# Residual gate rows: from VectorE products in the output projection to TensorE chunks in the projection stream

## The chip, the cores and the metric

The kernel runs on one core of a Trainium2 chip. The metric is the time of one execution on the device in microseconds (us); lower is better. The engines are named as in the profile: PE is TensorE (matmuls), DVE is VectorE, ACT is ScalarE, POOL is GpSimd, and SP is SyncE, which here only issues transfers (DMAs). SBUF is the on-chip memory, PSUM the memory that matmuls write, in eight banks.

## The reference

One layer of a hybrid diffusion backbone on 640 tokens (128 context, 512 latent) of 2048 features, all in float32:

```
mod   = silu(c) @ w_mod + b_mod              # 2048 -> 3 x 2048, for c (latent) and c_ctx (context)
shift, scale, gate = split(mod, 3)
h     = rms_norm(x, norm_w) * (1 + scale) + shift
proj  = h @ w_in                             # 640 x 2048 -> 640 x 7216
u_f, z_f, q, k, v, z_d, a, b = split(proj)
y_f   = fourier_mix(u_f) * silu(z_f)         # 4 groups of 128 channels
y_d   = rms_norm(gated_delta(conv(q), conv(k), conv(v), a, b)) * silu(z_d)   # 12 heads of 128, two directions
y     = concat(y_f, y_d) @ w_out             # 640 x 2048 -> 640 x 2048
out   = rms_norm(x + gate * y, final_norm_w)
```

The final states of the scan over the context tokens are an output too. What the change is about is `gate`: two rows of 2048 numbers, one for the latent and one for the context tokens, which are a vector times a third of `w_mod` (2048 x 2048, 16 MB) plus a bias. They are needed only at the very end, where they multiply the output projection.

## The kernel before

Matrices are cut into tiles of 128 partitions. The large products are made in float32r in three passes: each weight tile is split into a rounded part `whi` (ACT, line 135) and a rest `wlo` (POOL, line 136), each activation likewise, and PE computes hi x hi, lo x hi and hi x lo.

The work has four stages. At startup (lines 156 to 440) `x` is transposed and normed, and shift and scale are made by `mod_rows` (line 275): for each of 16 row blocks of `w_mod`, a matmul with 32 columns of weights `cz` (of which two are used, the two conditioning vectors) and 256 columns of `w_mod`, four such side by side in the four column strips of the array by `tile_position=(0, 32 * q)`. A second step adds the four strips.

The projection stream (`stream`, line 976) runs through 50 tiles of 128 columns of `w_in`, 2 x 48 matmuls of 320 tokens each (line 988). Between its chunks the program interleaves, by generators, the steps of the heads: `solve` (line 596) inverts the diagonal 32 x 32 blocks on DVE, with detours through DRAM (`pd`, `NP`, `xd`, `DD`); `delta` (line 701) puts together the whole 128 x 128 inverse and runs the scan with the state `S`; `head_out` multiplies by the gate of the branch; `fourier` does the Fourier groups. The generators are stepped against a clock written out by hand (lines 1284 to 1304): the stream adds 0.82 a step, and a generator yields a latency, after which it is due again, and a busy time. The order so given is a priority: the trace has loads for the next head issued as soon as their buffer is free.

In `delta`, one tile `AL` holds, for both directions and five chunks, the decayed products of keys (index 0, later the inverse) and of keys with queries (index 1). `DD` holds the inverted blocks, spread out over 128 columns with zeros between.

The output projection (`out_stream`, line 1219) has four column groups of 512 columns. Group `n` takes 16 row groups `k` of `w_out` and, for each of five token tiles, three matmuls of 512 columns (line 1252); the fourth group is cut into tokens 0 to 2 and 3 to 4, so that there are five passes, `p` 0 to 4. Pass 0 starts while the last heads finish. Five sums need five of the eight PSUM banks, so passes alternate between `bank` (five) and `mbank` (three). `out_loader` splits weights four row groups ahead; for the first three column groups they come through `raw`, issued by ACT, and for the fourth through `wo`, issued by SP into four buffers of the tag `wg`.

The gates are made here as well. `out_gate` (line 1098) loads, for each column group, four pieces of 1 MB of `w_mod` into the same tag `wg`, multiplies them on DVE by the two vectors, 32 products of 128 x 512 (lines 1108 and 1110), and splits the sums; `finish` adds over the partitions by a matmul with a matrix of ones, which also spreads the result over all partitions. Since the gates come later than the sums of the projection, groups 0 to 2 are copied out of PSUM to `res` by ACT (line 1274), and multiplied, added to `x` and squared later (`out_add`, line 1158), in an order that `out_gates` (line 1181) makes from an estimate of how far DVE has come.

Of the kernel before, what the change touches and what calls it, by code (L numbers as in the profile page):

```python
# [71 lines left out]
def hybrid_step(ctx: ExitStack, tc: tile.TileContext, x_prompt, x_sample, state_ctx, c, c_ctx,  # L72
# [28 lines left out]
    gd = dram.tile([24, NT], F32, name="gd")  # L101
    gb4 = dram.tile([NH, 4, 2, 160], F32, name="gb4")
# [133 lines left out]
        # The scale of the modulation comes first: the gate columns and the keys, values and queries of the first head  # L236
        # are multiplied without the shift, which the tokens share; its product with their columns is added later.
# [204 lines left out]
    # a first result comes back from DRAM, and the product with the shift is added  # L442
# [19 lines left out]
    def gates():  # L462
# [8 lines left out]
        ax, aa, au, lg = [g.tile(W24, F32, tag="ab", name="ab", bufs=4) for _ in range(4)]  # L471
# [48 lines left out]
    YT = g.tile([P, 5, 64], F32, tag="YT", name="YT")  # L520
    TA = g.tile([P, 5, 64], F32, tag="TA", name="TA")
    for x in (YT, TA):
        POOL.memset(x, 0.0)
# [58 lines left out]
    # gates wait in DRAM, in the place of the branch outputs that they will multiply  # L582
# [13 lines left out]
    def solve(h):  # L596
# [67 lines left out]
        YB = g.tile([40, 16, 16], F32, tag="YB", name="YB", bufs=1)  # L664
# [25 lines left out]
        for b in range(4):  # L690
            SP.dma_start(out=DD[32 * b:32 * b + 32, 0:2, :, 32 * b:32 * b + 32].rearrange("p d t c -> p (d t) c"),
                         in_=xd[10 * b:10 * b + 10].rearrange("u r c -> r u c"))
# [6 lines left out]
    LAT = (1, 2, 3, 4)  # L699

    def delta(h):
# [14 lines left out]
        AL = g.tile([P, 2, 5, 2, P], F32, tag="AL", name="AL", bufs=1)  # L716
        for ts in ((0, 1, 2), (3, 4)):
            pk = bank()
            for i, t in enumerate(ts):
                o = toff(t)  # L720
                PE.matmul(pk[:, P * i:P * (i + 1)], lhsT=KT[:, o:o + P], rhs=QT[:, o:o + P], start=True, stop=True)
            for i, t in enumerate(ts):
                E = g.tile([P, 2, P], F32, tag="E", name="E", bufs=2)
                for d in range(2):
                    ACT.activation(E[:, 1 - d], gb[:, d, P * t:P * (t + 1)], AF.Exp, bias=ngg4[:, d, h, t:t + 1])
                DVE.tensor_tensor(AL[:, :, t, 0], s["KK"][:, :, t], E, ALU.mult)
                DVE.tensor_tensor(AL[:, :, t, 1], pk[:, P * i:P * (i + 1)].unsqueeze(1).broadcast_to([P, 2, P]), E,
                                  ALU.mult)
# [5 lines left out]
        def half(x, odd):  # L734
            return x.rearrange("p (m b c) -> p m b c", m=2, b=2)[:, :, odd]

        px = bank()
        for t in range(5):
            for d in range(2):
                for m in range(2):  # L740
                    (o, co), (_, ci) = pairs[2 * m + 1 - d], pairs[2 * m + d]
                    PE.matmul(px[o, 32 * t:32 * t + 32], lhsT=AL[:, 1 - d, t, 0, co], rhs=DI[d][:, t, ci],
                              start=True, stop=True, tile_position=(0, o.start))
        for r, cc in pairs:
            POOL.tensor_copy(AL[r, :, :, 0, cc], DD[r, 1:3, :, cc])
        for b in range(4):
            POOL.tensor_copy(TA[pairs[b][0], :, pairs[b % 2][1]], DD[pairs[b][0], 0 if b < 2 else 3, :, pairs[b][1]])
        pv = px[:, 0:160].rearrange("p (t c) -> p t c", t=5)
        ACT.copy(YT[0:64, :, 0:32], pv[0:64])
        ACT.copy(YT[64:128, :, 32:64], pv[64:128])  # L750
# [6 lines left out]
        pv = px[:, 0:320].rearrange("p (t c) -> p t c", t=5)  # L757
        DVE.transpose(TA[32:64, :, 0:32], pv[0:32, :, 0:32])
        DVE.transpose(TA[64:96, :, 32:64], pv[96:128, :, 32:64])
        for d in range(2):  # L760
            for m in range(2):
                i, o, cc = pairs[2 * d + m][0], pairs[2 * m + d][0], pairs[2 * m + 1 - d][1]
                ACT.copy(AL[o, 1 - d, :, 0, cc], pv[i, :, 32 * m:32 * m + 32])
# [4 lines left out]
        for t in range(5):  # L768
            for d, (ra, rb) in enumerate(((lo, up), (up, lo))):
                PE.matmul(px[rb, 64 * t:64 * t + 64], lhsT=AL[ra, 1 - d, t, 0, rb], rhs=TA[ra, t, :], start=True, stop=True,  # L770
# [4 lines left out]
        for t in range(5):  # L775
            for d, (ra, rb) in enumerate(((lo, up), (up, lo))):
                PE.matmul(px[ra, 64 * t:64 * t + 64], lhsT=ET[rb, t, :], rhs=AL[rb, 1 - d, t, 0, rb], start=True, stop=True,
                          tile_position=(rb.start, ra.start))
        for d, (ra, rb, cp) in enumerate(((lo, up, DVE.tensor_copy), (up, lo, ACT.copy))):
            cp(AL[ra, 1 - d, :, 0, rb], px[ra, 0:320].rearrange("p (t c) -> p t c", t=5))  # L780
        yield 2.50, 1.1
        # scan: the context chunk, then the latent chunks in both directions
# [16 lines left out]
        for step in range(-1, 4):  # L799
# [24 lines left out]
            for d in range(2):  # L824
                PE.matmul(pv[:, P * d:P * (d + 1)], lhsT=AL[:, 1 - d, tt[d], 0, :],
# [19 lines left out]
            for d in range(2):  # L845
                PE.matmul(po[:, P * d:P * (d + 1)], lhsT=AL[:, 1 - d, tt[d], 1, :], rhs=vn[:, d], start=True, stop=True)
# [54 lines left out]
    def fourier(f):  # L901
# [4 lines left out]
        # 8-point transform over the grid rows  # L906
# [17 lines left out]
        # transform over the channels of the group: cosine and negative sine parts  # L924
# [8 lines left out]
        # transform over the context tokens, and over the grid columns  # L933
# [87 lines left out]
    # program order: projection chunks, and between them the steps of the heads and of the Fourier groups  # L1021
# [75 lines left out]
    # gate of a column group: products on the vector engine, the sum over the rows (and over all partitions) by ones  # L1097
    def out_gate(n):
        ns = slice(2 * DM + 512 * n, 2 * DM + 512 * n + 512)
        ga = [late.tile([P, 512], F32, tag=f"ga{m}", name="ga", bufs=1) for m in range(2)]  # L1100
        for j in range(4):
            wm = late.tile([P, 4, 512], F32, tag="wg", name="wg", bufs=4)
            SP.dma_start(out=wm, in_=wmv[:, 4 * j:4 * j + 4, ns])
            for q in range(4):
                for m in range(2):
                    cm = cz[:, 4 * j + q, m:m + 1]
                    if j + q:
                        DVE.scalar_tensor_tensor(ga[m], wm[:, q], cm, ga[m], ALU.mult, ALU.add)  # L1108
                    else:
                        DVE.tensor_scalar(ga[m], wm[:, q], cm, None, ALU.mult)  # L1110
                yield 1.32
        bg = late.tile([1, 512], F32, tag="gy", name="bg", bufs=2)
        SP.dma_start(out=bg, in_=b_mod[:, ns])
        parts = []
        for m in range(2):
            DVE.tensor_tensor(ga[m][0:1], ga[m][0:1], bg, ALU.add)
            gh = late.tile([P, 512], F32R, tag="gh", name="gh", bufs=2)
            gl = late.tile([P, 512], F32R, tag="gl", name="gl", bufs=2)
            ACT.copy(gh, ga[m])  # L1119
            DVE.tensor_tensor(gl, ga[m], gh, ALU.subtract)  # L1120
            parts.append((gh, gl))
            yield 1.8

        def finish():
            late.gate[n] = []
            for m, (gh, gl) in enumerate(parts):
                pg = bank()
                PE.matmul(pg, lhsT=late.ones, rhs=gh, start=True, stop=False)
                PE.matmul(pg, lhsT=late.ones, rhs=gl, start=False, stop=True)
                gt = late.tile([P, 512], F32, tag=f"gate{m}", name="gate", bufs=2)  # L1130
                ACT.copy(gt, pg)
                late.gate[n].append(gt)

        late.finish[n] = finish

# [4 lines left out]
    late.gate, late.wo, late.finish, late.got = {}, {}, {}, 0  # L1140
    LEAD, LAG = 3.0, 1.5

    def out_open():
        e = ctx.enter_context(tc.tile_pool(name="outp", bufs=1))
        late.tile = e.tile
        late.ones = e.tile([P, P], F32R, name="ones_r")
        ACT.copy(late.ones, K("ones"))
# [9 lines left out]
    # gating, residual, and the sum of squares of a column group  # L1157
    def out_add(t, n, y):
# [175 lines left out]
```

## Time and profile before

| | |
|---|---|
| three runs | 1521.86, 1523.84, 1523.9 us; median 1523.84 |
| profiled execution | span of its instructions 1520.9 us (no time beside the span is given for it) |
| PE busy | 1385.3 us, 91% |
| DVE busy | 1030.4 us, 68% |
| ACT, POOL busy | 655.0 us, 683.2 us |
| moved by DMA | 196.18 MB, mean 129 GB/s |

The page has a row of busy tenths by slices of the span, here that of DVE, 40 slices of 38 us:

```
DVE  4454347895969595867768585959583444599955
```

A group row of the page reads: line, engine, operation, output and inputs with shapes, count, busy time and mean ns of one, and after the last bar the idle time of the engine just before, with what ended it. A wait row reads: the waiting line, what it waited for, total us, times, longest. A timeline row: start, duration, engine, line. A row of windows: the stretch and its length, then PE, weight loads, DVE, ACT and POOL busy with counts, the granted PE clock, the DMA share and GB/s. Matmuls are pipelined, so that the distance between starts says more than a duration. A float32 matmul shows as two records.

### The profile page before, as it was taken

The numbers are of one execution on the slowest core, as the hardware profiler recorded it, in microseconds if no ns is written. First come the engines' busy times: TensorE is split into PE (matmuls) and PEld (weight loads), VectorE is DVE, ScalarE is ACT, GpSimd is POOL, SyncE is SP. The second block draws the span as 40 slices with busy tenths as digits, with TensorE's granted clock in tenths as the row PEclk, the third lists the DMA queues.
The fourth block names the chain that finished last, engine by engine and source line by source line (L and its number), as shares of the span: only waits on it lengthen the run. The fifth ranks groups of instructions, "written<-read, shape, count | busy, mean of one in ns | idle before, by whom it ended". The sixth has DMA issues, their size and how long they took to land. (4 is left out here: it accounts for less than half of the span.)

```text
span 1520.9 us, 26471 instructions
## 1 busy us (share of the span) xinstructions
PE 1385.3 (91%) x10052; PEld 1270.7 (84%) x10052; DVE 1030.4 (68%) x1698; ACT 655.0 (43%) x1717; POOL 683.2 (45%) x761
## 2 busy tenths in 40 slices
PE   6999999899898999999998989898999999979866
PEld 5676889788897999998998989898999988757655
DVE  4454347895969595867768585959583444599955
ACT  5344357236262626353544536262633433223234
POOL 2223336445354535354453544454435332364495
PEclk9999999899999999999999999999999999989989
DMA  9999434313233323233332323332324454855523
GB/s 303 295 335 310 150 120 125 88 44 108 63 85 86 86 74 92 77 90 86 89 87 70 92 81 99 85 96 69 98 77 125 135 166 141 302 186 158 174 77 139
DMA packets 242070, 196.18 MB, mean 129 GB/s; under 512 B 43117, under 2 KB 204826, under 8 KB 241814
## 3 DMA queue, kind: packets, MB, share of 16 engines
q1 hardware_dynamic: 121334, 122.65, 25.3%
q10 hardware_dynamic: 120608, 71.84, 16.9%
q8 instruction: 79, 1.29, 0.3%
q14 instruction: 49, 0.40, 0.1%
HBM read 170.47 MB, written 23.98 MB: 128 GB/s over the span
## 5 line engine op out<-in xcount | busy, mean ns | idle before, releaser
L136 POOL TENSOR_TENSOR wlo<-raw,whi 128x512 fp32r<-128x512 f32 (+1 forms) x276 | 395.9, 1441 | 576.3 <-ACT whi L135 457.8
L988 PE MATMUL mbank<-h_hi,whi 128*128 128x320 f32 x1600 | 520.2, 325 | 0.0
L988 PE MATMUL mbank<-h_lo,whi 128*128 128x320 f32 x1600 | 505.5, 316 | 0.0
L988 PE MATMUL mbank<-h_hi,wlo 128*128 128x320 f32 x1600 | 504.0, 315 | 0.0
L988 PEld LDWEIGHTS mbank<-h_hi,whi 128*128 128x128 f32 x1600 | 308.5, 193 | 2.7
L988 PEld LDWEIGHTS mbank<-h_lo,whi 128*128 128x128 f32 x1600 | 307.9, 192 | 0.5
L988 PEld LDWEIGHTS mbank<-h_hi,wlo 128*128 128x128 f32 x1600 | 307.1, 192 | 0.2
L135 ACT CAST whi<-raw 128x512 fp32r<-128x512 f32 (+1 forms) x276 | 167.7, 615 | 195.5 <-POOL wlo L136 50.7
L1108 DVE SCALAR_TENSOR_TENSOR ga<-wg,cz,ga 128x512 f32<-128x512 f32 x120 | 113.3, 1014 | 0.0
L670 DVE TENSOR_TENSOR tmp<-XB,YB 40x1024 f32<-40x1024 f32 (+1 forms) x60 | 107.7, 1796 | 1.3
L670 DVE TENSOR_TENSOR tmp<-NP,XB 40x1024 f32<-40x1024 f32 (+1 forms) x60 | 106.5, 1774 | 1.5
L820 POOL TENSOR_SCALAR kd<-k,edl 128x128 f32<-128x128 f32 x96 | 63.1, 669 | 50.5 <-PE bank L833 50.2
L1252 PE MATMUL bank<-wlo,y_hi 128*128 128x512 f32 x160 | 63.6, 398 | 13.0 <-POOL wlo L136 13.0
L1252 PE MATMUL mbank<-whi,y_hi 128*128 128x512 f32 x160 | 64.9, 406 | 9.7 <-ACT res L1274 7.1
L807 PE MATMUL bank<-S,KT 128*128 128x128 f32 x192 | 36.1, 301 | 39.9 <-DVE S L841 39.8
L548 ACT COPY pj<-mbank 128x128 f32<-128x128 f32 (+2 forms) x99 | 30.2, 340 | 90.8 <-PE mbank L988 49.7
L1252 PE MATMUL mbank<-wlo,y_hi 128*128 128x512 f32 x160 | 63.9, 399 | 5.4 <-POOL wlo L136 4.5
L807 PEld LDWEIGHTS bank<-S,KT 128*128 128x128 f32 x192 | 28.1, 194 | 46.3 <-DVE S L841 45.5
L1252 PE MATMUL bank<-whi,y_hi 128*128 128x512 f32 x160 | 63.8, 399 | 0.0
L1252 PE MATMUL mbank<-whi,y_lo 128*128 128x512 f32 x160 | 63.4, 396 | 0.0
L1252 PE MATMUL bank<-whi,y_lo 128*128 128x512 f32 x160 | 63.3, 396 | 0.0
L672 DVE TENSOR_REDUCE YB<-tmp 40x64 f32<-40x512 f32 (+2 forms) x60 | 59.8, 996 | 1.8
(327 smaller groups left out, 2578.2 us busy)
## 6 DMA issues: line engine op xcount, KB each, us to landing
raw<-in_w_in ACTq DMA_DIRECT2D x104, 512.0 KB
wm<-in_w_mod SPq DMA_DIRECT2D x64, 512.0 KB
wg<-in_w_mod SPq DMA_DIRECT2D x16, 1024.0 KB
raw<-in_w_out ACTq DMA_DIRECT2D x48, 256.0 KB
gb<-gd SPq DMA_DIRECT2D x12, 640.0 KB
yd<-zs SPq DMA_DIRECT2D x16, 320.0 KB
zl<-yd SPq DMA_DIRECT2D x16, 320.0 KB
yd<-zl SPq DMA_DIRECT2D x16, 320.0 KB
```

The costliest lines, as they stand in the source:

```text
L135: ACT.copy(whi, raw_part)
L136: sub.tensor_tensor(wlo, raw_part, whi, ALU.subtract)
L548: ACT.copy(pj[:, a:b], ps)
L670: DVE.tensor_tensor(tv, A.unsqueeze(2).broadcast_to(s4), B.rearrange("p j c -> p c j").unsqueeze(1).broadcast_to(s4), ALU.mult)
L672: DVE.tensor_reduce(dst, tv, AX.X, ALU.add)
L807: PE.matmul(pks[:, P * d:P * (d + 1)], lhsT=KT[:, a:a + P], rhs=S[:, d], start=True, stop=True)
L820: POOL.tensor_scalar(kd[:, d], k[:, tt[d], :], edl4[:, d, h, tt[d]:tt[d] + 1], 1.0, ALU.mult, ALU.mult)
L988: PE.matmul(pm[:, 0:320], lhsT=w, rhs=h[k][:, a:b], start=n == 0, stop=n == 3 * NK - 1)
L1108: DVE.scalar_tensor_tensor(ga[m], wm[:, q], cm, ga[m], ALU.mult, ALU.add)
L1252: PE.matmul(acc[t], lhsT=a[kk][:, sl], rhs=w, start=kk == order[0] and j == 0, stop=kk == order[-1] and j == 2)
```

## The change

The gates move into the projection stream. A new generator `res_gates`, started after the first head, computes them in eight parts of 256 columns with the matmuls of `mod_rows`, four at a time, each four followed by a DVE sum into `ga`; `sel_mod` adds the strips, the bias is added, and the two rows are stored to DRAM (`gates_d`). At the start of pass 1 all gates are loaded, spread over the partitions, into one tile `gate`; `x` is loaded into `res` for groups 1 to 3. `out_add` then works straight from PSUM at the end of passes 1 to 4; only group 0 is copied out, and gated during pass 1. `out_gate`, `out_add_of`, `out_gates` and `finish` go.

To make room for the new tiles, several others shrink or share: `DD` is stored packed (128 x 4 x 5 x 32 in place of 128 x 4 x 5 x 128), which turns the second product of the block inverse from 10 matmuls on 128 rows into 20 on 32 rows; the key half of `AL` is computed in place in `KK` (`T`), the query half becomes `AT` with two buffers; `YB` uses the buffer of `gr`, and the four tiles `ab` that of `tmp`.

```diff
+    def res_gates():
+        while ("delta", 0) not in done:
+            yield 4.00, 0
+        for i in range(8):
+            ns = slice(2 * DM + 256 * i, 2 * DM + 256 * i + 256)
+            ga = g.tile([P, 256], F32, tag="ga", name="ga", bufs=1)
+            for j in range(4):
+                gw = g.tile([P, 4, 256], F32, tag="gw", name="gw", bufs=1)
+                SP.dma_start(out=gw, in_=wmv[:, 4 * j:4 * j + 4, ns])
+                yield 9.00, 0
+                pg = bank()
+                for q in range(4):
+                    PE.matmul(pg[32 * q:32 * q + 32, 0:256], lhsT=cz[:, 4 * j + q, :], rhs=gw[:, q, :], start=True, stop=True,
+                              tile_position=(0, 32 * q))
+                if j:
+                    DVE.tensor_tensor(ga, ga, pg[:, 0:256], ALU.add)
+                else:
+                    DVE.tensor_copy(ga, pg[:, 0:256])
+            bt = g.tile([2, 256], F32, tag="gbt", name="gbt", bufs=1)
+            SP.dma_start(out=bt, in_=b_mod[0, ns].partition_broadcast(2))
+            yield 4.00, 0.5
+            pg = bank()
+            PE.matmul(pg[0:2, 0:256], lhsT=K("sel_mod"), rhs=ga, start=True, stop=True)
+            DVE.tensor_tensor(bt, bt, pg[0:2, 0:256], ALU.add)
+            SP.dma_start(out=gates_d[:, 256 * i:256 * i + 256], in_=bt)
+            yield 1.00, 0.5
...
-    live = [[x(), 0.0] for x in (outs, deltas, solves, fouriers)]
+    live = [[x(), 0.0] for x in (outs, deltas, solves, fouriers, res_gates)]
...
+    def out_add(t, n, y, weigh=True):
         ns = slice(512 * n, 512 * n + 512)
-        res, gate = late.res[t], late.gate[n][1 if t == 0 else 0]
+        res, gate = late.res[t], late.gate[:, n, 1 if t == 0 else 0]
         tmp = late.tile([P, 512], F32, tag="gy", name="gy", bufs=2)
-        if n < 3:
+        if n == 0:
             SP.dma_start(out=tmp, in_=xs[t][:, ns])
-            DVE.tensor_tensor(y, y, gate, ALU.mult)
+            DVE.tensor_tensor(res[:, ns], res[:, ns], gate, ALU.mult)
         else:
             DVE.tensor_tensor(tmp, y, gate, ALU.mult)
         DVE.tensor_tensor(res[:, ns], res[:, ns], tmp, ALU.add)
         ACT.activation(tmp, res[:, ns], AF.Square, scale=DM ** -0.5, accum_out=late.ssq[:, t, n:n + 1])
+        if weigh:
+            POOL.tensor_tensor(res[:, ns], res[:, ns], late.fnw[:, ns], ALU.mult)
...
             if p == 1:
-                SP.dma_start(out=late.fnw, in_=final_norm_w.partition_broadcast(P))
-                for t in range(5):
-                    SP.dma_start(out=late.res[t][:, 1536:2048], in_=xs[t][:, 1536:2048])
-                late.gs = out_gates()
-                next(late.gs)
+                for n2 in range(4):
+                    SP.dma_start(out=late.gate[:, n2], in_=gates_d[:, 512 * n2:512 * n2 + 512].partition_broadcast(P))
+                    if n2 == 0:
+                        SP.dma_start(out=late.fnw, in_=final_norm_w.partition_broadcast(P))
+                for n2 in range(1, 4):
+                    for t in range(5):
+                        SP.dma_start(out=late.res[t][:, 512 * n2:512 * n2 + 512], in_=xs[t][:, 512 * n2:512 * n2 + 512])
...
+                if p == 1 and 5 <= i < 10:
+                    out_add(i - 5, 0, None)
...
-            for t in toks:
-                if n < 3:
+            for t in (toks if p != 1 else (3, 4, 0, 1, 2)):
+                if n == 0:
                     ACT.copy(late.res[t][:, ns], acc[t])
-                    continue
-                out_add(t, n, acc[t])
-                if p < 4:
-                    POOL.tensor_tensor(late.res[t][:, ns], late.res[t][:, ns], late.fnw[:, ns], ALU.mult)
-            late.got = n + 1
+                else:
+                    out_add(t, n, acc[t], p < 4)
...
-    DD = g.tile([P, 4, 5, P], F32, tag="DD", name="DD")
-    POOL.memset(DD, 0.0)
+    DD = g.tile([P, 4, 5, 32], F32, tag="DD", name="DD")
...
-        AL = g.tile([P, 2, 5, 2, P], F32, tag="AL", name="AL", bufs=1)
+        T = s["KK"]
+        s["AT"] = AT = g.tile([P, 2, 5, P], F32, tag="AT", name="AT", bufs=2)
...
-                DVE.tensor_tensor(AL[:, :, t, 0], s["KK"][:, :, t], E, ALU.mult)
-                DVE.tensor_tensor(AL[:, :, t, 1], pk[:, P * i:P * (i + 1)].unsqueeze(1).broadcast_to([P, 2, P]), E,
+                DVE.tensor_tensor(T[:, :, t], T[:, :, t], E, ALU.mult)
+                DVE.tensor_tensor(AT[:, :, t], pk[:, P * i:P * (i + 1)].unsqueeze(1).broadcast_to([P, 2, P]), E,
                                   ALU.mult)
...
             for d in range(2):
-                PE.matmul(px[64 * d:64 * d + 64, 64 * t:64 * t + 64], lhsT=YT[:, t, :],
-                          rhs=half(DT[d][:, t, :], 1 - d), start=True, stop=True, tile_position=(0, 64 * d))
+                for m in range(2):
+                    i, o = pairs[2 * m + 1 - d][0], pairs[2 * d + m][0]
+                    PE.matmul(px[o, 32 * t:32 * t + 32], lhsT=YT[i, t, :], rhs=DT[d][i, t, :],
+                              start=True, stop=True, tile_position=(i.start, o.start))
```

More of the change, by code (lines that the diff above doesn't have):

```diff
@@ L470, in gates @@
         yield 3.00, 0.3
-        ax, aa, au, lg = [g.tile(W24, F32, tag="ab", name="ab", bufs=4) for _ in range(4)]
+        ab = g.tile([P, 4, 24, 5], F32, tag="tmp", name="ab", bufs=1)
+        ax, aa, au, lg = [ab[:, i] for i in range(4)]
         DVE.tensor_tensor(ax, pbv[:, 0:24, :], dtb.unsqueeze(2).broadcast_to(W24), ALU.add)
@@ L514, in hybrid_step @@
     gd2 = gd.rearrange("(d h) n -> h d n", d=2)
-    DD = g.tile([P, 4, 5, P], F32, tag="DD", name="DD")
-    POOL.memset(DD, 0.0)
+    DD = g.tile([P, 4, 5, 32], F32, tag="DD", name="DD")
     DI, DT = (DD[:, 0], DD[:, 3]), (DD[:, 2], DD[:, 1])
-    YT = g.tile([P, 5, 64], F32, tag="YT", name="YT")
+    YT = g.tile([P, 5, 32], F32, tag="YT", name="YT")
     TA = g.tile([P, 5, 64], F32, tag="TA", name="TA")
-    for x in (YT, TA):
-        POOL.memset(x, 0.0)
+    POOL.memset(TA, 0.0)
     XB = g.tile([40, 1056], F32, tag="XB", name="XB")
@@ L740, in delta @@
                 for m in range(2):
-                    (o, co), (_, ci) = pairs[2 * m + 1 - d], pairs[2 * m + d]
-                    PE.matmul(px[o, 32 * t:32 * t + 32], lhsT=AL[:, 1 - d, t, 0, co], rhs=DI[d][:, t, ci],
-                              start=True, stop=True, tile_position=(0, o.start))
+                    (o, co), (i, _) = pairs[2 * m + 1 - d], pairs[2 * m + d]
+                    PE.matmul(px[o, 32 * t:32 * t + 32], lhsT=T[i, 1 - d, t, co], rhs=DI[d][i, t, :],
+                              start=True, stop=True, tile_position=(i.start, o.start))
         for r, cc in pairs:
-            POOL.tensor_copy(AL[r, :, :, 0, cc], DD[r, 1:3, :, cc])
+            POOL.tensor_copy(T[r, :, :, cc], DD[r, 1:3])
         for b in range(4):
[L747 to L750, printed above, removed]
+            POOL.tensor_copy(TA[pairs[b][0], :, pairs[b % 2][1]], DD[pairs[b][0], 0 if b < 2 else 3])
+        ACT.copy(YT, px[:, 0:160].rearrange("p (t c) -> p t c", t=5))
         yield 2.50, 1.4
@@ L762, in delta @@
                 i, o, cc = pairs[2 * d + m][0], pairs[2 * m + d][0], pairs[2 * m + 1 - d][1]
-                ACT.copy(AL[o, 1 - d, :, 0, cc], pv[i, :, 32 * m:32 * m + 32])
+                ACT.copy(T[o, 1 - d, :, cc], pv[i])
         yield 3.00, 1.1
@@ L769, in delta @@
             for d, (ra, rb) in enumerate(((lo, up), (up, lo))):
-                PE.matmul(px[rb, 64 * t:64 * t + 64], lhsT=AL[ra, 1 - d, t, 0, rb], rhs=TA[ra, t, :], start=True, stop=True,
+                PE.matmul(px[rb, 64 * t:64 * t + 64], lhsT=T[ra, 1 - d, t, rb], rhs=TA[ra, t, :], start=True, stop=True,
                           tile_position=(ra.start, rb.start))
@@ L845, in delta @@
             for d in range(2):
-                PE.matmul(po[:, P * d:P * (d + 1)], lhsT=AL[:, 1 - d, tt[d], 1, :], rhs=vn[:, d], start=True, stop=True)
+                PE.matmul(po[:, P * d:P * (d + 1)], lhsT=AT[:, 1 - d, tt[d], :], rhs=vn[:, d], start=True, stop=True)
             for d in range(2):
@@ L958, in fourier @@
         yield 0.50, 0
+    def res_gates():
[24 more added lines that the diff above has]
+            yield 1.00, 0.5
+        done.add("res_gates")
     place = {"k": C_K, "v": C_V, "q": C_Q, "z": C_ZD, "u": 0, "f": 512}
@@ L1095, in out_loader @@
                     yield split(raw[:, q].rearrange("p (a b) -> p a b", a=4), DVE if q and len(toks) == 2 else POOL)
[L1098 to L1134, printed above, removed]
     class Late:
@@ L1139, in hybrid_step @@
     late = Late()
-    late.gate, late.wo, late.finish, late.got = {}, {}, {}, 0
-    LEAD, LAG = 3.0, 1.5
+    late.wo = {}
     def out_open():
@@ L1145, in out_open @@
         late.tile = e.tile
-        late.ones = e.tile([P, P], F32R, name="ones_r")
-        ACT.copy(late.ones, K("ones"))
+        late.gate = e.tile([P, 4, 2, 512], F32, name="gate")
         late.fnw = e.tile([P, DM], F32, name="fnw")
@@ L1168, in out_add @@
         ACT.activation(tmp, res[:, ns], AF.Square, scale=DM ** -0.5, accum_out=late.ssq[:, t, n:n + 1])
-    def out_add_of(n):
-        ns = slice(512 * n, 512 * n + 512)
-        for t in range(5):
-            out_add(t, n, late.res[t][:, ns])
-            POOL.tensor_tensor(late.res[t][:, ns], late.res[t][:, ns], late.fnw[:, ns], ALU.mult)
-            yield 1.4
-        if n == 2:
-            DVE.tensor_reduce(late.ssum, late.ssq[:, :, 0:3], AX.X, ALU.add)
-            DVE.tensor_scalar(late.ssum, late.ssum, EPS, None, ALU.add)
-    def out_gates():
-        t_pe = t_dve = 0.0
-        gens, n, wait = [out_gate(0)], 0, {}
-        while gens or wait or n < 4:
-            for m in [m for m in wait if t_pe > wait[m] + LAG and (m == 3 or late.got > m)]:
-                del wait[m]
-                late.finish[m]()
-                if m < 3:
-                    gens.insert(0, out_add_of(m))
-            if gens and t_dve < t_pe + LEAD:
-                cost = next(gens[0], None)
-                if cost is None:
-                    done_one = gens.pop(0)
-                    if n in late.finish and n < 4:
-                        wait[n] = t_dve
-                        n += 1
-                        if n < 4:
-                            gens.append(out_gate(n))
-                    continue
-                t_dve = max(t_dve, t_pe) + cost
-            else:
-                t_pe += (yield)
+        if weigh:
+            POOL.tensor_tensor(res[:, ns], res[:, ns], late.fnw[:, ns], ALU.mult)
     def out_norm(t, last):
@@ L1259, in out_stream @@
                     out_norm(i // 3, False)
[L1260 to L1264 removed]
+                if p == 1 and 5 <= i < 10:
+                    out_add(i - 5, 0, None)
             if p == 0:
                 yield "opened"
[L1267 to L1279 removed]
+            for t in (toks if p != 1 else (3, 4, 0, 1, 2)):
+                if n == 0:
+                    ACT.copy(late.res[t][:, ns], acc[t])
+                else:
+                    out_add(t, n, acc[t], p < 4)
+            if p == 2:
+                DVE.tensor_reduce(late.ssum, late.ssq[:, :, 0:3], AX.X, ALU.add)
+                DVE.tensor_scalar(late.ssum, late.ssum, EPS, None, ALU.add)
             if p == 4:
```

34 lines of the change are left out of this document (10 added, 24 removed).

## The prediction

> **What bounds the kernel now.** I read the page first, then TensorE's waits in the output projection, then the chain that ended last, and only then single instructions.
>
> ```profile
> span 1520.9 us, 26471 instructions
> ...
> PE 1385.3 (91%) x10052; PEld 1270.7 (84%) x10052; DVE 1030.4 (68%) x1698; ACT 655.0 (43%) x1717; POOL 683.2 (45%) x761
> ...
> L1108 DVE SCALAR_TENSOR_TENSOR ga<-wg,cz,ga 128x512 f32<-128x512 f32 x120 | 113.3, 1014 | 0.0
> ```
>
> TensorE (PE) is busy for 91% of the span, so by the average it is the bound, and a change that gives it more work should cost time. But the 113.3 us of the gate products on VectorE (DVE, line 1108) do not lie spread over the span; they lie in its last seventh. So the stage has to be read by itself. These are PE's waits from 1277 us on:
>
> ```profile
> PE bank L1252 <- POOL wlo L136: 13.0, 2, 10.9
> PE bank L1128 <- ACT gh L1119: 8.9, 2, 8.7
> PE mbank L1252 <- ACT res L1274: 7.1, 1, 7.1
> PE mbank L1252 <- POOL wlo L136: 4.5, 3, 2.0
> PE mbank L1252 <- ACT whi L135: 2.7, 1, 2.7
> ```
>
> And this is the chain of waits behind the longest of them (10.9 us), in order of time:
>
> ```profile
> 1439.31 4.78 DVE ga L1108 x8
> ...
> 1446.22 3.66 DMA wo<-in_w_out
> ...
> 1449.91 0.74 DVE ga L1108
> ...
> 1452.00 3.98 DMA wo<-in_w_out
> 1455.97 2.50 POOL wlo L136 x2
> ```
>
> The reader is to see that the releaser named first, POOL's `wlo`, is only the messenger. POOL waited for the weights `wo`; their load waited for a buffer of the tag `wg`; that buffer was held by the gate products on DVE. The 8.7 us wait is for `gh`, which is made from the same sums, and the 7.1 us wait is for ACT, whose queue stands behind such a `gh` (line 1119). In this stage DVE bounds the kernel and PE waits for it.
>
> How much PE loses there comes from four starts:
>
> ```profile
> 1289.52 0.39 PE L1252 MATMUL mbank<-whi,y_hi 128*128 128x512 f32 x1
> ...
> 1292.92 0.39 PE L1252 MATMUL mbank<-whi,y_hi 128*128 128x512 f32 x1
> ...
> 1296.32 0.39 PE L1252 MATMUL bank<-whi,y_hi 128*128 128x512 f32 x1
> ...
> 1510.14 0.39 PE L1252 MATMUL mbank<-whi,y_lo 128*128 128x512 f32 x1
> ```
>
> The first two are the same matmul of two successive row groups, 15 matmuls apart: 3.40 us, or 0.2267 us each when nothing waits. The third is the first matmul of pass 1, the fourth the last of the kernel. Passes 1 to 4 have 16 x (15 + 15 + 9 + 6) = 720 matmuls, so 719 steps: 163.0 us at that rate, where they took 213.8. The excess is **50.8 us**: 36.2 us of the five waits above, the 16 matmuls by `ones`, and steps at a low clock after the gaps.
>
> **The change, part by part.**
>
> *Removed at the end.* 120 products, 8 first products, the hi/lo splits of the sums, the 16 `ones` matmuls and the 16 loads of 1 MB that share buffers with `wo`. `wo` has its four buffers to itself, so the chain above is gone. What is late next? `out_add` now stands at the end of each pass. Its prices:
>
> ```profile
> L1164 DVE TENSOR_TENSOR res<-res,gate 128x512 f32<-128x512 f32 x15 | 9.5, 676 | 0.0
> ...
> L1278 POOL TENSOR_TENSOR res<-res,fnw 128x512 f32<-128x512 f32 x3 | 4.6, 1523 | 0.5 <-ACT gy L1168 0.5
> ...
> PE mbank L1252 <- POOL wlo L136: 2.0, 1, 2.0
> PE mbank L1252 <- DVE wlo L136: 0.9, 1, 0.9
> ```
>
> At the start of pass 3, POOL has five `fnw` products (5 x 1.52 = 7.6 us, about 2 us after the pass ends: two DVE steps of 0.68 and a square) and then the fifth row group's `wlo` (1.25 by the chain's last line), 10.9 us in all; PE has four row groups ready, 4 x 9 x 0.2267 = 8.2 us. It waits 2.7 us. The last two rows are PE's waits from 1485 us on, in pass 4, where little changes: 2.9 us stay. At the start of pass 2 the banks of tokens 3 and 4 are emptied by DVE and not by ACT, about 0.6 us. The gates come back broadcast (4 loads of 512 KB) on SP ahead of `fnw` (1 MB) and 15 loads of 256 KB; the first `out_add` comes five row groups (17 us) into pass 1, and PE waits for none of it before row group 10. So 6.2 us of the 50.8 stay and **44.6 us** go. Bounds: 50.8 if nothing is late, 25 if POOL's burst or the loads hold a pass for some 20 us more.
>
> *Added in the projection stream.* After the first head, `res_gates` takes 32 steps: a load of 512 KB on SP, four matmuls of 32 columns of weights on PE, one DVE sum. The trace has such a group among wide matmuls, at startup:
>
> ```profile
> 61.29 0.34 PE L265 MATMUL bank<-h_hi,wlo 128*128 128x384 f32 x1
> 61.46 0.29 PE L266 MATMUL mbank<-h_hi,wlo 128*128 128x256 f32 x1
> 61.59 0.34 PE L265 MATMUL bank<-h_hi,whi 128*128 128x384 f32 x1
> 61.86 0.64 PE L278 MATMUL mbank<-wm,cz 128*32 128x256 f32 x8
> 62.43 0.39 PE L266 MATMUL mbank<-h_hi,whi 128*128 128x256 f32 x1
> 62.65 0.34 PE L265 MATMUL bank<-h_lo,whi 128*128 128x384 f32 x1
> 63.83 0.38 PE L286 MATMUL mbank<-cst,ms 128*128 128x128 f32 x2
> ```
>
> Four matmuls are eight records. From one L265 to the next but one takes 0.30 us without the group (61.29 to 61.59) and 1.06 with it (61.59 to 62.65): the group costs 0.76 us, and 32 cost 24.3. The eight sums by `sel_mod` are nearest to the last row, with twice its columns: 0.38 to 0.76, 0.45 taken, 3.6 together. PE gets **28 us** more work.
>
> [...]
>
> Not all of the 28 us lands where PE is the bound:
>
> ```profile
> 390.00:420.00 30.00, 25.05 (x166) 23.70 (x164) 28.52 (x39) 9.23 (x30) 13.12 (x13) 0.94 0.26 67
> ...
> 450.00:480.00 30.00, 26.12 (x176) 25.67 (x175) 27.56 (x37) 6.92 (x18) 10.28 (x8) 0.94 0.19 58
> ...
> 540.00:570.00 30.00, 26.93 (x175) 26.67 (x174) 29.48 (x33) 7.66 (x18) 11.62 (x11) 0.89 0.26 75
> ...
> 630.00:660.00 30.00, 24.02 (x164) 23.39 (x164) 26.54 (x36) 7.07 (x17) 12.74 (x14) 0.94 0.33 90
> ...
> 345.00:745.00 400.00, 368.98 (x2929) 356.75 (x2928) 298.77 (x494) 184.78 (x531) 188.97 (x237) 0.97 0.31 85
> ...
> PE bank L807 <- DVE S L841: 39.8, 20, 3.2
> L727 DVE TENSOR_TENSOR AL<-bank,E 128x256 f32<-128x256 f32 x60 | 24.6, 417 | 13.9 <-PE bank L721 13.8
> L695 DVE STREAM_TRANSPOSE DD<-DD 128x1280 f32<-128x1280 f32 x12 | 18.0, 1503 | 4.4 <-DMA DD<-xd 4.3
> ```
>
> Of the eleven stretches of 30 us from 360 to 690 us, in which most groups will fall, these four are the ones with DVE busy for over 26 of 30 us (third number with a count), and PE idles 3.1 to 6.0 there, 17.9 in all: there DVE is the bound, and PE waits for the state `S` (the wait row, of the whole stream). 4/11 of 28, 10 us, disappears in that idle time. But the DVE sums land there too: 40 of 0.42 us (L727 is the nearest, 256 columns from PSUM), 16.8 us, 4/11 of it 6 us. The diff also packs `DD`: the transpose of line 695 shrinks from 1280 to 320 elements, from 1.50 to some 0.5 us, 12 times, 12 us; it stands in the path at the change of heads only in part, so I count a third, 4 us. The other edits (`YB` in the buffer of `gr`, `T` in place of `KK`, two `AT`, 20 matmuls on 32 rows for 10 on 128) I cost at nothing: their PE work is under 1 us per head, and the load of `gr` has a whole head's time; if that cover goes, a head's solve starts by a DMA latency later (4.3 us, next rows).
>
> The new waits:
>
> ```profile
> SPq L643 <- DVE g L640: 48.6, 5, 10.4
> 1276.90 0.32 SPq L1074 DMA_DIRECT2D yt<-yd  x1
> 1281.21 0.73 ACT L1077 CAST y_hi<-yt 128x640 fp32r<-128x640 f32 x1 [0.90 <-DMA yt<-yd]
> ```
>
> `gw` has one buffer, so SP waits until PE has read it, then loads; the program leaves 9 units of its clock (about 10 us) until the next group. 320 KB took 4.3 us; 512 KB is 4.3 to 6.9. That leaves 3 to 5 us. SP's queue is often stuck behind DVE (first row, 350 to 700 us: 10.4 us at worst), and if the load goes out that late, the group waits in PE's queue with the whole projection (line 988) behind it, and the sum waits in DVE's with the solve and scan behind it. The `b_mod` load and the store of the gates (8 each) have nobody waiting for hundreds of us. Bounds 0 to 32 x 5 us. PE and DVE wait for each other at every step of the scan, and PE's wait for `S` is 3.2 us at most, so DVE and SP's queue behind it should lag PE by less than the slack: I take 3 us.
>
> Stream: 28 - 10 + 6 - 4 + 3 = **23 us**. All: -44.6 + 23 = -21.6. The page gives the profiled execution's span, 1520.9; that becomes 1499.3. The runs' median, 1523.84, lies 2.9 above the span, which I leave as it is: **1502 us**, own range 1490 to 1515.
>
> **Rivals.**
>
> *The stream takes the gate work almost free.* PE idles 31 us of the 400 that the groups will take (row 345 to 745), and two `AT` and the short transpose smooth the change of heads. Then the stream costs 5, not 23: 1523.8 - 44.6 + 5 = 1484. Against it: 17.9 of the 31 lie in the four stretches that I have counted already.
>
> *PE waits for the gate weights (slower).* The moved loads land late, and each group halts the projection. It decides from 21.6 / 32 = 0.7 us a group. Half the groups late by 4 us, about one latency, cost 64 us in place of 3: 1563; a third of them late by 4, 1542. For it: SP's waits and the single buffer. Against it: the load is the first thing behind the group before it, and the lag by the row of `S` is short.
>
> *The output stage stays fed badly.* POOL's burst of `fnw` products, or the 7 MB of loads at its start, becomes its bound, and only 25 us go: 1522, no change. For it: POOL's steps take 1.5 us each and stand ahead of `wlo`. Against it: outside the burst a row group needs one `wlo` per 3.4 us.
>
> That the gates are not done in the stream, so that they delay the end, I exclude: 8 x 42 clock units are some 370 us from 345 us on, and the stream runs to 1277.
>
> **How the numbers follow.** Forecast 0.54, free stream 0.20, late weights 0.15, badly fed 0.08, else 0.03. A measurement of this kernel can tell 0.2%, 3 us, from no change. Faster: 0.54, 0.20, 0.03 of the badly fed and a rest of 0.02: 0.79. Slower: late weights 0.13 and a rest of 0.01, 0.14. Same: 0.07, from badly fed and mild lateness. The range reaches from just below the free stream to just above the badly fed case, 1480 to 1524; the late weights (0.14) and a little at the low end stay out.
>
> **What would show it.** Right: no 128x512 products on DVE at the end; PE's waits there 5 to 9 us in place of 36; the time from the first matmul of pass 1 to the last near 169 us; last matmul to the end about 11 us as now; the projection longer by some 23 us, the groups 0.76 us apart from their neighbours. Wrong: PE waits on `gw` of over 20 us in the stream, passes over 180 us, or a stream that is not longer.

## The result, and the profile after

The kernel after takes 1529.26 us (median of 13 runs, 1525.83 to 1538.39), the kernel before 1522.36 us beside it (13 runs, 1518.85 to 1525.9). The ratio is 1.0056, with a 95% interval of 1.0039 to 1.0072: slower by 0.56%, 6.9 us between the medians, where 1502 us had been forecast.

The page of the kernel after, in the lines that answer to those of before:

```profile
span 1526.2 us, 27377 instructions
...
PE 1407.7 (92%) x10548; PEld 1270.9 (83%) x10548; DVE 882.6 (58%) x1594; ACT 635.1 (42%) x1678; POOL 643.5 (42%) x759
...
DVE  4455257586867677394756748394856534422025
```

DVE has lost 148 us of work, and its last five slices, 99955 before, read 22025. PE has 22 us more. The stage at the end did what was forecast. Here is the stretch from the first matmul of pass 1 to the last, first in the kernel before, then in the kernel after (columns as in the row of windows described above; the eighth is the granted clock of PE):

```profile
1296.00:1510.00 214.00, 176.72 (x738) 141.66 (x737) 174.84 (x195) 66.50 (x131) 125.87 (x76) 0.93 0.50 170
```

```profile
1349.00:1515.00 166.00, 163.16 (x718) 134.42 (x717) 44.52 (x51) 52.83 (x104) 97.13 (x76) 1.00 0.38 132
```

PE no longer waits there for anything that hangs on the gate products. All of its waits from 1290 us on, in the kernel after:

```profile
PE mbank L1208 <- POOL wlo L137: 2.0, 1, 2.0
PE mbank L1208 <- DVE wlo L137: 0.9, 1, 0.9
PE bank L940 <- ACT A L929: 0.3, 1, 0.3
```

And the first matmul of pass 1 and the last of the kernel, in its timeline:

```profile
1349.00 0.39 PE L1208 MATMUL bank<-whi,y_hi 128*128 128x512 f32 x1
...
1515.46 0.39 PE L1208 MATMUL mbank<-whi,y_lo 128*128 128x512 f32 x1
```

That is 166.5 us where it was 213.8: **47.3 us won** (44.6 forecast). But pass 1 begins 52.7 us later than before. All of the loss, and more, lies in the projection stream.

To see where, I took from both traces the start of each of the 50 tiles of 96 stream matmuls (lines 988 and 1015). Tiles are counted from 0, and 50 stands for the last matmul of the stream. The table has those starts less the start of the same tile before, in us; the gate groups run from tile 7 to tile 21.

```
tile          9    12    16    20    23 |  24    28    32    36    40    44    50
after       0.8  18.0  21.6  30.2  32.0 | 36.0  40.0  43.7  47.8  50.4  53.0  52.8
```

Two things are to be seen. While the gates are computed, 32 us are lost. Then, with no gate work left at all, 2.6 to 4.1 us more go at each fourth tile, where one head gives way to the next: 21 us in six steps. Between those tiles next to nothing is lost (tile 27 still stands at 35.8). PE's waits from 690 us on, the groups over, first in the kernel before, then in the kernel after:

```profile
PE bank L807 <- DVE S L841: 23.4, 11, 3.2
PE bank L833 <- ACT vn L828: 2.4, 4, 0.6
PE bank L825 <- ACT TY L947: 0.3, 1, 0.3
```

```profile
PE bank L805 <- DVE S L839: 20.6, 11, 3.1
PE bank L768 <- DVE TA L756: 6.2, 6, 1.0
PE bank L768 <- DVE TA L757: 5.9, 6, 1.0
PE bank L831 <- ACT vn L826: 3.0, 5, 0.6
PE bank L753 <- ACT YT L746: 2.6, 6, 0.6
```

Three of the waits, one on `YT` and two on `TA`, come six times each, once a head, and the kernel before has none of them. They are in the block inverse. One such place, tile 27 to 28, on ACT, DVE and PE of the kernel after:

```profile
794.73 0.40 ACT L726 ACTIVATE E<-gb,ngg 128x128 f32<-128x128 f32 x1 [2.25 <-POOL gb L714]
795.04 2.67 ACT L627 ACTIVATE KK<-bank,ns 128x128 f32<-128x128 f32 x10
...
798.04 0.37 ACT L746 COPY YT<-bank 128x160 f32<-128x160 f32 x1
...
801.12 0.83 ACT L550 ACTIVATE vT<-pj,cw 128x641 f32<-128x641 f32 x1
```

```profile
792.71 0.16 DVE L617 TENSOR_TENSOR ns<-nbeta,rk 128x10 f32<-128x10 f32 x1
...
801.99 1.34 DVE L551 SCALAR_TENSOR_TENSOR vT<-pj,cw,vT 128x641 f32<-128x641 f32 x1 [1.02 <-ACT vT L550]
803.36 0.34 DVE L756 STREAM_TRANSPOSE TA<-bank 32x160 f32<-32x160 f32 x1
803.73 0.89 DVE L552 SCALAR_TENSOR_TENSOR vT<-pj,cw,vT 128x641 f32<-128x641 f32 x1
804.65 0.35 DVE L757 STREAM_TRANSPOSE TA<-bank 32x160 f32<-32x160 f32 x1
```

```profile
798.46 0.55 PE L753 MATMUL bank<-DD,YT 32*32 32x32 f32 x40 [0.39 <-ACT YT L746]
...
803.75 0.33 PE L768 MATMUL bank<-TA,KK 64*64 64x64 f32 x2 [1.03 <-DVE TA L756]
805.06 0.93 PE L768 MATMUL bank<-TA,KK 64*64 64x64 f32 x18 [0.98 <-DVE TA L757]
805.92 0.63 PE L1015 MATMUL mbank<-h_hi,whi 128*128 128x320 f32 x1
...
811.00 0.80 PE L775 MATMUL bank<-KK,ET 64*64 64x64 f32 x20
```

The same place in the kernel before, ACT and then PE:

```profile
755.79 2.69 ACT L627 ACTIVATE KK<-bank,ns 128x128 f32<-128x128 f32 x10
...
763.71 0.70 ACT L725 ACTIVATE E<-gb,ngg 128x128 f32<-128x128 f32 x2 [0.53 <-POOL wlo L136]
```

```profile
766.59 0.80 PE L770 MATMUL bank<-TA,AL 64*64 64x64 f32 x20
767.32 0.41 PE L988 MATMUL mbank<-h_hi,whi 128*128 128x320 f32 x1
...
771.03 0.80 PE L777 MATMUL bank<-AL,ET 64*64 64x64 f32 x20
```

In the kernel before, ACT makes the ten copies `KK` of the next head (line 627) first and its exps `E` eight us later. In the kernel after, one exp stands ahead of the copies. It waits 2.25 us for POOL to mask `gb`; the ten copies, whose last input `ns` was ready at 792.87, stand behind it until 795.04, and behind them the copy to `YT` and the activation for `vT`. DVE waits for `vT` (1.02), and its two transposes to `TA` stand behind the sums of `vT` (lines 551 and 552), so PE waits twice. Then PE's granted clock falls to 0.50, from 805.57 to 808.98 us: from the first of the 24 stream matmuls after the inverse step to the next step takes 811.00 - 805.92 = 5.08 us, where it took 771.03 - 767.32 = 3.71. So 0.39 + 1.03 + 0.98 + 1.37 = 3.8 of the 4 us.

The source has no such difference. The copies stand in `solve`, the exps in `delta`, with the same yields in both kernels. Which goes first on ACT is settled when the kernel is built.

### The profile page after: what moved, and what is told of

It reads as the page before. It is cut to its first block, busy times and chain, and to the rows that moved or that the text cites. A ratio compares the mean times of both kernels' runs of the same rounds, so it can differ in the third digit from the quotient of the medians.

```text
span 1526.2 us, 27377 instructions
## 1 busy us (share of the span) xinstructions
PE 1407.7 (92%) x10548; PEld 1270.9 (83%) x10548; DVE 882.6 (58%) x1594; ACT 635.1 (42%) x1678; POOL 643.5 (42%) x759
## 5 line engine op out<-in xcount | busy, mean ns | idle before, releaser
L137 POOL TENSOR_TENSOR wlo<-raw,whi 128x512 fp32r<-128x512 f32 (+1 forms) x276 | 382.1, 1389 | 583.1 <-ACT whi L136 481.1
L670 DVE TENSOR_TENSOR tmp<-NP,XB 40x1024 f32<-40x1024 f32 (+1 forms) x60 | 109.9, 1832 | 1.3
L818 POOL TENSOR_SCALAR kd<-k,edl 128x128 f32<-128x128 f32 x96 | 59.8, 634 | 41.6 <-PE bank L831 41.4
L726 ACT ACTIVATE E<-gb,ngg 128x128 f32<-128x128 f32 x120 | 42.2, 394 | 51.8 <-DVE AT L728 31.6
L672 DVE TENSOR_REDUCE XB<-tmp 40x64 f32<-40x512 f32 (+2 forms) x60 | 59.7, 995 | 1.3
```

The costliest lines, as they stand in the source:

```text
L137: sub.tensor_tensor(wlo, raw_part, whi, ALU.subtract)
L670: DVE.tensor_tensor(tv, A.unsqueeze(2).broadcast_to(s4), B.rearrange("p j c -> p c j").unsqueeze(1).broadcast_to(s4), ALU.mult)
L672: DVE.tensor_reduce(dst, tv, AX.X, ALU.add)
L818: POOL.tensor_scalar(kd[:, d], k[:, tt[d], :], edl4[:, d, h, tt[d]:tt[d] + 1], 1.0, ALU.mult, ALU.mult)
```

## The experiments

There were two theories at the outset, A and B; C came with e3, D with e7. **A**: the new layout of the inverse (packed `DD`, `T` in place of `KK`, twice the small matmuls) shifts the queues of ACT and POOL and costs 4 us a head. **B**: the gate work itself costs the 53 us of the stream, directly and by pushing the heads out of step. **C**: the order of exp and copies on ACT costs 4 us a head, and the gate groups have a price of their own beside it. **D**: the late loads of the gate weights are the cause of everything, and the order only follows them.

The first experiment, e1, was to move the gates alone and keep the old layout. It has no time: its tiles need 110.1 kb per partition where 105.3 are left. So what the gates cost with the old layout stays unmeasured.

### e2: the layout alone

The kernel before with all the edits to `DD`, `YT`, `AL`, `AT`, `YB` and `ab`; the gates stay on DVE.

```diff
-        AL = g.tile([P, 2, 5, 2, P], F32, tag="AL", name="AL", bufs=1)
+        T = s["KK"]
+        s["AT"] = AT = g.tile([P, 2, 5, P], F32, tag="AT", name="AT", bufs=2)
...
-    DD = g.tile([P, 4, 5, P], F32, tag="DD", name="DD")
+    DD = g.tile([P, 4, 5, 32], F32, tag="DD", name="DD")
```

> The kernel before with the new layout of the delta rule alone (DD packed, T in place in KK, two AT, 20 products on 32 rows, YB in the buffer of gr, ab in that of tmp); the gates stay on VectorE in the output projection. Theory A: the stream grows by some 3 to 4 us a head in 11 heads, 35 to 40 us, the output stage is as before, the kernel takes about 1560 us (1550 to 1565). Theory B: the layout costs nothing, about 1523 us, or some us less for the shorter transpose.

Measured: 1525.08 us beside 1522.78, ratio 1.0013 (0.9998 to 1.0028). The stream ends 1.8 us later than before, with no steps at the heads. Theory A, which gave 1550 to 1565, falls: the layout by itself costs about 2 us, which is not clear of none.

### e3: the exps held behind the copies

The kernel after, with one rule of order:

```diff
-                    ACT.mul(KK[:, 1 - d, t], pk[:, P * i:P * (i + 1)], s["ns3"][:, d, t:t + 1])
+                    s["KKi"] = ACT.mul(KK[:, 1 - d, t], pk[:, P * i:P * (i + 1)], s["ns3"][:, d, t:t + 1])
...
-                    ACT.activation(E[:, 1 - d], gb[:, d, P * t:P * (t + 1)], AF.Exp, bias=ngg4[:, d, h, t:t + 1])
+                    with tc.issue_after(s["KKi"].ins):
+                        ACT.activation(E[:, 1 - d], gb[:, d, P * t:P * (t + 1)], AF.Exp, bias=ngg4[:, d, h, t:t + 1])
```

> The changed kernel with one rule of order added: on ACT, the exponentials E of a head stand behind the ten copies KK of the same head (whose product with E is what needs them). No work is added or left out. Theory C (the changed program makes a list order in which one E of the next head stands ahead of the KK copies on ACT, waits there for POOL's mask on gb, and so delays YT, the transposes on VectorE and the third product of the inverse on TensorE; some 4 us a head for the heads behind the gates): the seven boundaries from tile 19 on lose their 4 us each, the time falls by 20 to 28 us to about 1504 us. Theory B (the moved gate work is what costs the 53 us): about 1529 us, no change.

Measured: 1514.31 us beside 1523.95, ratio 0.9939 (0.9922 to 0.9956). Tile 23 starts 38.9 us later than before, and the stream ends 40.1 us later: the steps after the groups are gone (1.2 us from tile 23 on, 20.8 in the kernel after). The time is 15 us below the 1529.26 of the kernel after, short of the 20 to 28 forecast: its tile 23 starts 6.9 us later than in the kernel after. Of these, 4.3 are there at the start of tile 7, ahead of the first group, where the order of exps and copies is the same in both kernels; the rest is open.

### e4 and e5: no gate work, without and with the rule

```diff
...
-            ga = g.tile([P, 256], F32, tag="ga", name="ga", bufs=1)
-            for j in range(4):
...
             bt = g.tile([2, 256], F32, tag="gbt", name="gbt", bufs=1)
-            SP.dma_start(out=bt, in_=b_mod[0, ns].partition_broadcast(2))
...
+            SP.dma_start(out=bt, in_=b_mod[0, 2 * DM + 256 * i:2 * DM + 256 * i + 256].partition_broadcast(2))
+            yield 41.0, 0
...
```

This is e4; e5 has the rule of e3 besides.

> The changed kernel with the gate groups left out: no loads of gate weights, no matmuls and no sums in the stream; the rows stored as gates are the bias alone, so the residual is gated with wrong numbers. All else as in the changed kernel. Its order on ACT has an E ahead of KK from about the fifth head on, as the changed kernel's has. Theory C: the output stage is 47 us shorter, the stream still pays some 4 us at each of the later boundaries, 25 to 30 us, the time is about 1502 us. Theory B: without gate work the stream is as in the kernel before, the time is 1477 us.

> The same without gate work, and with the order of the first kernel of this call (E behind KK); the residual is gated with the bias alone. Theory C: the stream is within 5 us of that before, the time is 1475 to 1482 us, and what is left to the first kernel of this call is the price of the gate groups themselves, 22 to 30 us. Theory B: the same as without the rule of order.

Measured: e4 1506.98 us, ratio 0.989 (0.9859 to 0.9921), and e5 1484.5 us in a single run. Both are some us above what theory C gave. The stream ends 34.8 us later than before in e4, 7.7 in e5. Theory B falls: without any gate work 27 us of the stream's loss stay (22.5 between the two times), and they go with the order. PE's waits from 690 us on in e4:

```profile
PE bank L805 <- DVE S L839: 21.9, 14, 3.1
PE bank L768 <- DVE TA L756: 6.2, 6, 1.0
PE bank L768 <- DVE TA L757: 5.9, 6, 1.0
```

The same two lines of `TA`, to the tenth, with no gate work in the kernel.

### e6, e7 and e8: the gate weights

What is left of e3 against e5 is 32 us of span. e6 is e3 with the gate weights loaded once, ahead of all groups (so all groups multiply the same rows); e7 is the kernel after with two buffers, e8 is e3 with two:

```diff
-                gw = g.tile([P, 4, 256], F32, tag="gw", name="gw", bufs=1)
+                gw = g.tile([P, 4, 256], F32, tag="gw", name="gw", bufs=2)
```

> E behind KK, and the gate weights loaded once in place of 32 times (all groups multiply the same piece, so the gates are wrong): the matmuls and the sums stay, the loads and SP's waits for them go. If the loads cost the stream through TensorE's waits for them (4.9 us in four waits, and a low clock after each), it is 5 to 12 us faster than the kernel with the order alone. If they cost nothing beside the groups, it is the same within 3 us.

> The kernel after, with two buffers for gw in place of one, so that a load no longer waits for the group before it; nothing else is changed, and on ACT the first exp of a head still stands ahead of the ten KK copies from the fifth head on. Theory C (the order on ACT and the gate groups are two separate prices): PE's waits on gw (4.9 us and more at the change of heads) go, 4 to 9 us of the 1529 are won, 1520 to 1525, about the kernel before, and the stream still falls back by 4 us per head after the groups are over. Rival D (the late loads are the cause of everything, the order only follows them): 1506 to 1511.

> As e3 (exps of a head held behind its KK copies), with two buffers for gw. Theory C: e3's 1514 less the 4 to 9 us of the loads, 1505 to 1510, near the 1508 of one look at a single load of the gate weights; 13 to 16 us below e7. Rival D: the same time as e7 within 3 us.

Measured: e6 1507.78 us in a single run, 6.5 below e3; e7 1526.66 us beside 1522.29, ratio 1.002 (1.0001 to 1.004); e8 1502.66 us, ratio 0.988 (0.9859 to 0.9901). e8 beats both kernels. Rival D falls, since e7 and e8 differ by 1.4% with the same buffers. Theory C's figures were missed by little: e7 is 1.7 us above its 1520 to 1525, e8 2.3 us below its 1505 to 1510. Against the kernel before, the second buffer takes the ratio from 1.0056 to 1.002 without the rule, and from 0.9939 to 0.988 with it, some 5 and 9 us. Each ratio is known to about 0.2%, so whether the two prices simply add is not shown. This is the wait that goes, first from the kernel after, then from e3, between 340 and 700 us:

```profile
PE bank L971 <- DMA gw<-in_w_mod: 4.9, 4, 2.4
```

```profile
PE bank L972 <- DMA gw<-in_w_mod: 7.1, 5, 3.0
```

Of the four waits of the kernel after one alone, 2.02 us at 445.68, was followed by a low clock (0.50 from 447.17 to 450.58 us), not each as was expected for e6. In e7 and e8 the list of PE's waits has no `gw`. Tile 23 of e7 starts no earlier for it (32.7 us later than before, 32.0 in the kernel after): the list of the same stretch has 4.6 us for `KT` and 3.3 for `o`, where the kernel after has none and 0.7. But the trace of e7 is that of its slowest run of ten, 1532.83 us, and why these waits came is not settled.

A group by itself costs what was forecast. e8's timeline:

```profile
472.01 0.31 PE L1016 MATMUL mbank<-h_hi,wlo 128*128 128x320 f32 x1
472.25 0.64 PE L972 MATMUL bank<-gw,cz 128*32 128x256 f32 x8
472.81 0.41 PE L1016 MATMUL mbank<-h_hi,whi 128*128 128x320 f32 x1
473.06 0.30 PE L1016 MATMUL mbank<-h_lo,whi 128*128 128x320 f32 x1
473.21 0.31 PE L1016 MATMUL mbank<-h_hi,wlo 128*128 128x320 f32 x1
```

Two steps from 472.01 to 473.06 take 1.05 us; two steps without a group take 2 x 0.147 (the last two rows are 0.15 apart). That leaves 0.76 us, and the 14 groups of e8 that stand whole between two pairs of stream matmuls all give 0.76 or 0.77. The next matmul starts 0.56 us after the group's start, within its 0.64.

### e9 and e10: the good order without a rule

If the order alone is the cause, it needs no rule, only a kernel that happens to be built in the other order. e9 is e4 without its generator, which there only moved the bias:

```diff
+    for _m in range(2):
+        SP.dma_start(out=gates_d[_m:_m + 1], in_=b_mod[:, 2 * DM:3 * DM])
...
-    live = [[x(), 0.0] for x in (outs, deltas, solves, fouriers, res_gates)]
+    live = [[x(), 0.0] for x in (outs, deltas, solves, fouriers)]
```

e10 is e7 with one number changed:

```diff
-                yield 9.00, 0
+                yield 8.00, 0
```

> As e4 (no gate work; the gate rows are only the bias), but the generator res_gates is left out altogether, and the bias is stored by two DMAs ahead of the stream; no rule on the exps. The order of the KK copies and the exps on ACT is then that of the kernel before in every head. Theory C (that order costs 4 us a head): the time of e5, 1482 to 1490, some 22 us below e4, though e4 has only 16 small DMAs more. Rival (e5 gained by something else in its rule, or the new layout has a price of its own beside the order): 1500 to 1507, as e4.

> As e7 (all gate work, two buffers for gw), but each group follows its load after 8.00 units of the program's clock rather than 9.00; no rule on the exps. From the seventh head on the KK copies then stand ahead of the exps. Theory C: near e8, 1500 to 1508, 18 to 24 us below e7. Rival (the rule of e3 and e8 gained by something else than this order): within 4 us of e7, 1521 to 1530.

Measured: e9 1482.53 us beside 1523.56, ratio 0.9712 (0.9686 to 0.9737); e10 1505.15 us, ratio 0.9885 (0.9868 to 0.9901). Both as theory C has it: 24.5 us below e4, and 21.5 below e7. The waits from 690 us on, e9 and then e10:

```profile
PE bank L805 <- DVE S L839: 22.1, 15, 3.1
PE bank L831 <- ACT vn L826: 3.0, 5, 0.6
```

```profile
PE bank L805 <- DVE S L839: 23.1, 15, 3.1
PE bank L823 <- DVE r L808: 5.8, 4, 1.8
PE bank L831 <- ACT vn L826: 2.3, 4, 0.6
PE bank L768 <- DVE TA L756: 1.0, 2, 0.6
```

And ACT at the place shown above, in e10: the copies again come first.

```profile
784.17 2.69 ACT L627 ACTIVATE KK<-bank,ns 128x128 f32<-128x128 f32 x10 [0.43 <-DVE ns L617]
...
791.02 0.68 ACT L726 ACTIVATE E<-gb,ngg 128x128 f32<-128x128 f32 x2
```

In the kernel after, e4 and e7 one exp stands ahead of the copies in each of the last six heads; in all the others it does in none of these six. The rule of e3 asks for this order alone, and with it the six steps are gone; whether the builds of e9 and e10 differ from e4 and e7 in other orders too was not compared.

All kernels side by side: how much later than before tile 23 starts and the stream ends (tile 50), the time from the first matmul of pass 1 to the last, and the span of the profiled execution (us). Each row is one execution, and those of one kernel differ by up to 15 us (e7: 1517.4 to 1532.83):

```
                                    tile 23  tile 50  passes 1-4   span
before                                    0        0       213.8  1520.9
after                                  32.0     52.8       166.5  1526.2
e2  layout alone                        2.9      1.8       212.1  1520.7
e3  after, rule                        38.9     40.1       167.2  1514.2
e4  no gate work                       14.8     34.8       166.4  1508.4
e5  no gate work, rule                  6.5      7.7       168.0  1482.3
e6  rule, one load                     28.4     31.3       166.5  1505.7
e7  after, two buffers                 32.7     54.2       168.8  1531.0
e8  rule, two buffers                  28.9     30.1       168.3  1507.2
e9  no gate work, no generator          9.7      9.0       166.5  1481.9
e10 two buffers, yield 8               24.4     28.5       166.4  1502.6
```

## Why the prediction was wrong

- **The bound at the end** was right: DVE was the limit of the last seventh, and 47.3 us went (44.6 forecast). Of the 6.2 us of waits that were to stay, 2.9 came, the two rows of `wlo` in pass 4; the 2.7 us for POOL's burst in pass 3 and the 0.6 at the start of pass 2 did not. From the last matmul's start to the end it is 10.7 us, 10.8 before.
- **The gate groups** were right in size: 0.76 us each. With absorption and DVE sums, 28 - 10 + 6 = 24 were forecast; e10 less e9 gives 28.5 - 9.0 = 19.5 (22.6 between the medians), e8 less e5 30.1 - 7.7 = 22.4.
- **The waits on `gw`** were 4.9 us in the trace (3 forecast). The rival that made the kernel slower by late gate weights needed over 20; it has the right sign, but not the cause.
- **The sum for the stream**, 28 - 10 + 6 - 4 + 3 = 23, is the step that failed: what it takes for the change of heads. There it had -4 for the transpose and nothing for `YB`, `T`, the two `AT` and the 20 matmuls, because their work is small. The work is indeed small: the layout alone costs 2 us (e2), and the transpose went from 1503 to 504 ns, as forecast. What the sum put at nothing without a reason is that edits to what is issued in the stream can change the order in which the engines' queues are filled. Here they did, and in the kernel after that order costs 2.6 to 4.1 us at each of six changes of heads, 21 us, all behind the last group, where no gate work is left. Four pairs of kernels, with the order as their main difference, agree. Their times differ by 22.5 (e4 and e5), 24.5 (e4 and e9), 24.0 (e7 and e8) and 21.5 us (e7 and e10). At the end of the stream the traces differ by 27.1, 25.8, 24.1 and 25.7 us, of which 18.8, 20.7, 20.3 and 17.4 arise behind tile 23, some 3 us a head. The rest arises earlier: in e4 the head at tile 20 has an exp ahead as well, and single executions differ by some us ahead of the first group already.
- **A smaller miss**: e5 and e9, without gate work and in the good order, end the stream 7.7 and 9.0 us later than before, where -4 was forecast. It arises between tiles 9 and 11, and e2 has 2 us of it. What makes the rest is open.

The sum of the terms as measured, by the traces of e9, e10 and the kernel after: 9.0 for the rest of the edits, 19.5 for the gate work, and 24.3 between e10 and the kernel after, which is the order and what one buffer costs; 52.8 in all, which they make by construction. With the good order e8 and e10 come to 1502.66 and 1505.15 us, beside the forecast of 1502: in e10 the output stage is 2.8 us better than its term and the stream 5.5 us dearer than 23. That these come so near to 1502 is partly luck, since the rest of the edits cost 9.0 where -4 stood, and the gate work 19.5 where 24 and 3 stood. It was the missing term that turned the sign. None of the signs named for being wrong came up: they asked for waits on `gw`, slow passes or a stream that is not longer, and not for one that is longer by more than 23 us.

Why the build falls into one order or the other is open. It does not take gate work (e4 has none), and the layout alone does not bring it (e2); the generator with its 16 small DMAs (e4 and e9) or one unit of the program's clock (e7 and e10) decided it; from the seventh head on each of these kernels keeps the one order or the other to its end.

## What to carry to other kernels

When a stream is interleaved by priorities, an edit that only adds work can have two prices: the work, and the order that the engines' queues fall into. Compare the starts of equal pieces of the stream in both traces: a loss that recurs where the added work is absent points to an order, and the first instruction at that place that waits with ready work behind it is the one to suspect. Confirm it by a rule that changes this order alone, and fix it so before judging the change by its time.

## What the runs showed of the hardware

In the trace of the kernel after, the granted clock changes only at times that lie whole multiples of 3.41 us apart, at 805.57 us for one. At five of the six changes of heads behind the groups it was 0.50 for 3.41 us, right after PE's two waits on `TA`. These are such windows, three around the place shown above (tile 28), then two at the change of heads at tile 40:

```profile
802.16:805.57 3.41, 1.40 (x22) 1.00 (x22) 3.28 (x6) 1.28 (x4) 0.65 (x4) 1.00 0.86 212
805.57:808.98 3.41, 3.41 (x19) 3.29 (x16) 1.11 (x2) 2.78 (x8) 0.00 (x0) 0.50 0.07 13
808.98:812.39 3.41, 3.41 (x38) 3.15 (x38) 0.48 (x1) 0.62 (x1) 1.27 (x1) 1.00 0.00 0
1058.15:1061.57 3.42, 1.87 (x13) 1.47 (x11) 2.56 (x3) 1.35 (x4) 1.29 (x1) 1.00 0.73 201
1061.57:1064.98 3.41, 2.95 (x33) 2.89 (x34) 2.01 (x5) 3.29 (x10) 0.17 (x3) 1.00 0.33 52
```

The waits of 1.03 and 0.98 us lie in the first window, which has 1.40 us of work, and no wait there was longer; the next window has a granted clock of 0.50. That is the 1.4 us (5.08 - 3.71) of the step at tile 28. At tile 40 PE waits 1.02 and 0.98 us, but a window ends at 1061.57, within the second wait: 1.87 us of work fall in the first, and the clock stays at 1.00. Over this whole trace, the 19 windows at full clock in which PE was busy for up to 47% were followed by half clock, the 402 with 49% or more were not. In the kernel before, cut the same way, these are 19 with up to 43% and 393 with 46% or more, so no single figure parts them in both traces; what decides the clock is not shown.
